# An earlier first modulation round and normed input inside the memory projection of a two-block kernel

## The chip, the cores and the metric

The kernel runs on one core of a Trainium2 chip. The metric is the device time of one execution in microseconds (us). Five engines work side by side and meet only at semaphores: TensorE (PE in the rows, its weight loads as PEld), VectorE (DVE), ScalarE (ACT), GpSimd (POOL) and SyncE (SP), which here only issues DMAs. The issue of a DMA shows as SPq, ACTq or POOLq.

## The reference, cut to what matters

Two transformer-like blocks on 512 positions of width 1024. What the change touches is the start of block 1 and a piece of block 2 that doesn't depend on block 1:

```python
cond = silu(c)
mod = cond @ ada_w + ada_b                       # 6 rows of 1024: sh1, sc1, g1, sh2, sc2, g2
u = rms_norm(x, mix_pre_g) * (1.0 + sc1) + sh1   # 512 x 1024, the mixer's normed input
proj = u @ w_in                                  # convolution branch first: a, gate
y = causal_dwconv(a * sigmoid(gate), cv_dw_w)    # 31 taps
...
m = rms_norm(mem, mem_norm_g)                    # block 2: 256 memory tokens
kv = m @ cross_w_kv                              # 1024 x 2048: keys and values of the cross-attention
```

All weights are float32. Products keep nearly float32 accuracy with three matmuls in a reduced type: a weight and an activation are each split into a high part and the low rest, and high by high, high by low and low by high are added up.

## The kernel before, in words

The first stage of the program is `memory` (L426, phase name `mem`). It reads the memory's weight `w_kv` in 16 chunks of 512 KB, c0 to c15 here, in four units of four chunks. A chunk is loaded by `weight` (L131): SP loads it into a buffer `raw` (three of them), ScalarE casts the high part (L140), VectorE subtracts for the low part (L146), both into a buffer of tag `whl` (four of them). Then TensorE does 12 matmuls of 128x512 (`mm3`, L151 to L153). L151 needs the high part of the weight; in this stage L152 is the one that needs its low part. After units 0 and 1 TensorE also transposes the keys (L486, tile `kn`), and each unit's result goes to DRAM by a DMA on POOL's queue (L498, `kvd`).

After each chunk the function `weave` (L538) is called with the chunk's number. It places the preparation of the mixer among the chunks:

- One step of `ada_round(0, ...)` (L236), the first modulation round: two tiles of 512 KB of `ada_w` (`aw`, four buffers, so two steps' worth) are loaded by SP and multiplied on TensorE in four small fp32 matmuls (L254; eight in the trace). There are eight steps, r0 to r7. After r7 VectorE adds `ada_b` (L257).
- `x_load(tb)` (L509): one of four blocks of x is loaded by SP, ScalarE sums its squares (L207), VectorE and POOL take the root, VectorE scales it (L515), TensorE transposes it (L520) and it is put into `xT`.
- `norm1()` (L528): transposes of the modulation (`mod_cols`, L264), then for each of eight slices of the features a scaling on VectorE (L534), a cast to the high part on ScalarE (L193) and the low part on VectorE (L194). The result is `u`, split; in the rows it is `mem_U`.

Next comes the mixer (L630), phase `glu`: 16 weight chunks g0 to g15 of `w_in`, each a `weight` and 24 matmuls in `fm_tile` (L215). In the mixer `lowdma` is set, and `weight` takes another way to the low part: ScalarE casts the high part (L140), writes minus the high part (L142), and a DMA on POOL's queue adds the raw weight to that (L143). Only when this accumulating DMA has landed is the low part there, and only then is the `raw` buffer free. In `fm_tile` it is L153 that needs the low part. A round of modulation for later use (`glu_U`) is woven into this phase too, and the 31-tap convolution runs on VectorE behind it.

The order of instructions on each engine is not the order of the source: a scheduling framework orders them by its own model of durations, and decides which buffer of a tag a tile gets. On an engine the order is then fixed, and what waits holds up everything behind it. SP's queue is one such order: a load that waits for its buffer holds up the loads behind it.

```python
ada = self.ada_round(0, lambda: pz.tile([P, 1024], F32, tag="aw", bufs=4, ...))   # L524
...
mm(out, lh, rh, start=start, stop=False)     # L151
mm(out, lh, rl, start=False, stop=False)     # L152
mm(out, ll, rh, start=False, stop=stop)      # L153
...
nc.scalar.activation(w[:, 1], raw, AF.Copy, scale=-1.0)            # L142, in the mixer
nc.gpsimd.dma_start(out=w[:, 1], in_=raw, accum_op=ALU.add)        # L143
```

Of the kernel before, what the change touches and what calls it, by code (L numbers as in the profile page):

```python
# [46 lines left out]
class Kern:  # L47
# [15 lines left out]
    def setup(self):  # L63
        nc, tc, ctx = self.nc, self.tc, self.ctx
        self.p0 = ctx.enter_context(tc.tile_pool(name="p0", bufs=1))
        self.psp = ctx.enter_context(tc.tile_pool(name="psp", bufs=4, space=PSUM))
        self.dr = ctx.enter_context(tc.tile_pool(name="dr", bufs=1, space=bass.MemoryType.DRAM))
        self.cols = self.p0.tile([P, self.a["cols"].shape[1]], F32, tag="cols", name="cols")
        nc.sync.dma_start(self.cols, self.a["cols"])
        self.ident = self.p0.tile([P, P], F32, tag="ident", name="ident")  # L70
        make_identity(nc, self.ident)
        self.ones = self.p0.tile([P, P], F32, tag="ones", name="ones")
        nc.vector.memset(self.ones, 1.0)
        self.half = self.p0.tile([P, 4], F32, tag="half", name="half")
        nc.vector.memset(self.half, -0.5)

        self.p0.tile([P, 8], F32, tag="mcol", bufs=2, name="mcol")
        self.p0.tile([P, 8], F32, tag="cvec", name="cvec")
        self.p0.tile([P, 8], F32, tag="cond", name="cond")
        self.p0.tile([P, 112], F32, tag="gap0", name="gap0")  # L80
# [142 lines left out]
    def ada_setup(self):  # L223
        nc = self.nc
        c = self.p0.tile([P, 8], F32, tag="cvec", name="cvec")
        nc.sync.dma_start(c, self.a["c"])
        cond = self.cond = self.p0.tile([P, 8], F32, tag="cond", name="cond")
        nc.scalar.activation(cond, c, AF.Silu)
        self.misc = self.p0.tile([P, 2048], F32, tag="misc", name="misc")
        self.crep = self.misc[:, 1024:1280].rearrange("p (k c) -> p k c", k=8)  # L230
        self.sin = self.misc[:, 1280:1664].rearrange("p (t f) -> p t f", t=4)
        self.cos = self.misc[:, 1664:2048].rearrange("p (t f) -> p t f", t=4)
        nc.vector.tensor_copy(self.crep, cond.unsqueeze(2).to_broadcast([P, 8, 32]))
        self.mods = {}
# [266 lines left out]
    def block1(self):  # L501
        nc, tc, a = self.nc, self.tc, self.a
        self.ada_setup()
        with tc.tile_pool(name="pz", bufs=1) as pz:
            self.phase = "mem"
            xT = self.U(F32)
            xs, xi = [], []

            def x_load(tb):  # L509
                t = pz.tile([P, 1024], F32, tag="x", bufs=2, name=f"x{tb}")  # L510
                nc.sync.dma_start(t, a["x"][tb * P:(tb + 1) * P, :])
                ss = self.small(1)
                self.sumsq(t, ss)
                rs = self.rsqrt(ss, D)
                nc.vector.tensor_scalar(t, t, rs, None, op0=ALU.mult)  # L515
                for i in range(2):
                    ps = self.psB()
                    for k in range(4):
                        kk = i * 4 + k
                        nc.tensor.transpose(ps[:, k * P:(k + 1) * P], t[:, kk * P:(kk + 1) * P], self.ident)  # L520
                    (nc.scalar.copy if i else nc.vector.tensor_copy)(
                        xT[:, i * 4:i * 4 + 4, 0, tb * P:(tb + 1) * P], ps.rearrange("p (k t) -> p k t", k=4))

            ada = self.ada_round(0, lambda: pz.tile([P, 1024], F32, tag="aw", bufs=4, name=self.nm("aw")))  # L524

            u = self.U()

            def norm1():  # L528
                self.phase = "norm1"
                sh1 = self.mod_col8(0, 0)  # L530
                g1 = self.mod_col8(0, 1, "mix_pre_g")
                for k in range(8):
                    t = self.tB()
                    nc.vector.tensor_scalar(t, xT[:, k, 0], g1[:, k:k + 1], sh1[:, k:k + 1], op0=ALU.mult, op1=ALU.add)  # L534
                    self.split(u[:, k, 0], u[:, k, 1], t)
                self.phase = "mem"

            def weave(i):  # L538
                if i in (0, 2, 3, 5, 7, 9, 11, 13):
                    next(ada, None)  # L540
                if i in (3, 5, 7, 9):
                    x_load((3, 5, 7, 9).index(i))
                if i == 15:
                    norm1()

            self.memory(pz, weave)
        with tc.tile_pool(name="pa", bufs=1) as pa:
            mix, g1row, sh2, g2p = self.mixer(pa, u)
        with tc.tile_pool(name="pf", bufs=1) as pf:
            self.phase = "wout"  # L550
            self.pf = pf
            u2 = pf.tile([P, 8, 2, 512], F32R, tag="U2", name="u2")
            self.xs = []
            for tb in range(4):
                t = pf.tile([P, 1024], F32, tag="x4", bufs=6, name=self.nm("x"))
                nc.sync.dma_start(t, a["x"][tb * P:(tb + 1) * P, :])
                self.xs.append(t)
            self.xd = self.dr.tile([S, D], F32, tag="xd", bufs=2, name=self.nm("xd"))

            def after(tbs, ps):  # L560
                self.spill(tbs)
                return self.prenorm(tbs, self.xs, u2, ps, gcol=g2p, shcol=sh2)

            self.fin = self.post(g1row, after)
            for later in mix:
                pass
            self.phase = "up"
            act = self.ffn(pf, u2, later)
            self.phase = "down"
            self.rope_tables()  # L570
            self.clear_rows()
            g2row = self.mod_row(pf.tile([P, 1024], F32, tag="row1", name="g2row"), 2, 1, "ffn_post_g")
            an = self.row(pf, "attn_norm_g", tag="row2")
            xt = pf.tile([P, 8, 1024], F32, tag="U2", name="xt")
            self.xs = [xt[:, tb] for tb in range(4)]
            for tb in range(4):
                nc.sync.dma_start(self.xs[tb], self.xd[tb * P:(tb + 1) * P, :])
            self.xd = self.dr.tile([S, D], F32, tag="xd", bufs=2, name=self.nm("xd"))
            self.hA = None

            def after(tbs, ps):
                if self.hA is None:
                    self.hA = self.U()
                self.spill(tbs)
                return self.prenorm(tbs, self.xs, self.hA, ps, grow=an)

            for self.later in self.wide_product(act, "ffn_down", NFF, (((0, 1), 0, 8), ((0,), 8, 22), ((1,), 8, 22)),
                                                self.post(g2row, after)):
                pass
# [1606 lines left out]
```

## Time and profile before

| what | us |
|---|---|
| median of 3 runs (lowest, highest) | 1535.51 (1530.5, 1536.32) |
| the profiled execution, its own time | 1530.15 |
| its span, first to last instruction | 1528.4 |
| TensorE busy in the span | 1459.3 |
| VectorE, ScalarE, GpSimd busy | 958.8, 671.2, 124.4 |

The span is a little shorter than the execution's time, since launch and end lie around it. All stages named above lie in the first 100 us of the span; the rest of the program (mixer, feed-forward, attention, experts) follows them one after the other. Times of rows count from the span's start. A row of the timeline has the start, the duration, the engine, the line, the operation with what it writes and reads, how many instructions were merged, and in brackets how long the engine had been idle and what released it. Matmuls are pipelined, so their distance is shorter than the duration a row shows.

### The profile page before, as it was taken

The page shows a single profiled execution, that of the slowest core. Times are in us where ns is not written, and L with a number is a line of the kernel's source. Part 1 is how long each engine was busy: PE and PEld are TensorE (multiplying, and loading weights), DVE is VectorE, ACT ScalarE, POOL GpSimd, SP SyncE. Part 2 cuts the span into 40 slices and gives each one's busy share as a digit, 9 for nine tenths or more (in the row PEclk, how much of TensorE's full clock was granted, in tenths as well). Part 3 has the DMA queues.
Part 4 walks back from the last instruction along what each step waited for, and adds up shares of the span by engine and source line. Part 5 has one row for each costly group of instructions (what it writes and reads, how often), then busy time and mean ns, then how long its engine had stood idle before and what let it go on. Part 6 is the DMA issues. An engine that isn't in the chain of part 4 may idle for free.

```text
span 1528.4 us, 19917 instructions
## 1 busy us (share of the span) xinstructions
PE 1459.3 (95%) x7096; PEld 1083.4 (71%) x7096; DVE 958.8 (63%) x2099; ACT 671.2 (44%) x1212; POOL 124.4 (8%) x152
## 2 busy tenths in 40 slices
PE   7989999999999999999999999999999998999886
PEld 5667778778788788888888877878878785333322
DVE  4569999994866866565524778775676557332114
ACT  5553486576755754444324554454354421111010
POOL 0111111111000000000000010000011001111100
PEclk9999999999999999999999999999999999999999
DMA  9899977876376553333425633242343667999997
GB/s 333 308 287 270 272 183 189 225 193 151 111 262 206 179 194 96 97 96 97 145 90 193 200 125 111 93 163 90 97 151 102 232 250 283 416 412 412 409 410 282
DMA packets 95767, 321.66 MB, mean 210 GB/s; under 512 B 13129, under 2 KB 13641, under 8 KB 95664
## 3 DMA queue, kind: packets, MB, share of 16 engines
q1 hardware_dynamic: 80832, 276.39, 51.4%
q0 software_dynamic: 11952, 35.56, 10.5%
q10 hardware_dynamic: 2880, 8.39, 1.4%
q8 instruction: 57, 0.93, 0.2%
q14 instruction: 46, 0.38, 0.1%
HBM read 275.83 MB, written 26.74 MB: 198 GB/s over the span
## 4 chain that ended last, share of the span: by engine, by line
PE 69%; DMA 15%; DVE 9%; ACT 3%; issue 2%; POOL 2%; SPq 0%; ACTq 0%; DVEq 0%; POOLq 0%
PE up_pa L152 5%; PE up_pa L153 5%; PE up_pa L151 5%; PE glu_pa L151 2%; PE glu_pa L152 2%; PE vo_pa L151 2%; PE glu_pa L153 2%; PE vo_pa L153 2%; PE vo_pa L152 2%; PE wout_pa L153 2%; PE wout_pa L151 2%; PE wout_pa L152 2%; DMA wo_U<-in_w_dn_dram 2%; DMA crossq_U<-in_w_gu_dram 2%; DMA moe_U<-in_w_gu_dram 2%
## 5 line engine op out<-in xcount | busy, mean ns | idle before, releaser
L648 DVE SCALAR_TENSOR_TENSOR y<-g,cols,y 128x493 f32<-128x493 f32 (+26 forms) x240 | 165.7, 729 | 5.5 <-ACT y L645 3.8
L152 PE MATMUL up_pa<-u,up_w 128*128 128x512 f32 (+1 forms) x384 | 142.6, 372 | 0.4 <-DVE u L194 0.4
L151 PE MATMUL up_pa<-u,up_w 128*128 128x512 f32 (+1 forms) x384 | 142.3, 372 | 0.3 <-ACT u L193 0.3
L153 PE MATMUL up_pa<-u,up_w 128*128 128x512 f32 (+1 forms) x384 | 142.5, 372 | 0.0
L936 DVE SCALAR_TENSOR_TENSOR up_tA<-up_pa,cols,up_tA 128x511 f32<-128x511 f32 x88 | 65.8, 749 | 72.2 <-ACT up_tA L934 70.8
L151 PEld LDWEIGHTS up_pa<-u,up_w 128*128 128x128 f32 x384 | 72.1, 188 | 13.7 <-ACT u L193 1.1
L152 PEld LDWEIGHTS up_pa<-u,up_w 128*128 128x128 f32 x384 | 72.3, 188 | 13.0 <-DVE u L194 0.6
L153 PEld LDWEIGHTS up_pa<-u,up_w 128*128 128x128 f32 x384 | 72.3, 188 | 12.5
L146 DVE TENSOR_TENSOR down_w<-down_raw,down_w 128x1024 fp32r<-128x1024 f32 x36 | 42.8, 1220 | 55.3 <-ACT down_w L140 55.3
L1782 DVE COPY moe_xT<-moe_pb 128x512 f32<-128x512 f32 x15 | 10.4, 691 | 105.7 <-PE moe_pa L1896 105.3
L146 DVE TENSOR_TENSOR wout_w<-wout_raw,wout_w 128x512 fp32r<-128x512 f32 (+1 forms) x72 | 51.3, 745 | 35.2 <-ACT wout_w L140 35.0
L140 ACT CAST down_w<-down_raw 128x1024 fp32r<-128x1024 f32 x36 | 36.6, 1051 | 64.2 <-PE down_pb L153 33.0
L140 ACT CAST wout_w<-wout_raw 128x512 fp32r<-128x512 f32 (+1 forms) x72 | 44.8, 670 | 44.2 <-PE wout_pa L153 23.7
L934 ACT ACTIVATE up_tA<-up_pa,cols 128x512 f32<-128x512 f32 x44 | 34.4, 781 | 67.8 <-PE up_pa L153 67.7
L1898 ACT ACTIVATE moe_sl<-moe_pa,moe_gt 128x256 f32<-128x256 f32 x16 | 7.6, 474 | 124.1 <-PE moe_pa L1896 124.1
L151 PE MATMUL glu_pa<-mem_U,glu_w 128*128 128x512 f32 x128 | 51.6, 406 | 3.8 <-ACT mem_U L193 3.8
L146 DVE TENSOR_TENSOR up_w<-up_raw,up_w 128x1024 fp32r<-128x1024 f32 (+1 forms) x48 | 54.0, 1127 | 0.1
L152 PE MATMUL glu_pa<-mem_U,glu_w 128*128 128x512 f32 x128 | 51.4, 403 | 0.4 <-DVE mem_U L194 0.4
L152 PE MATMUL g_pa<-g_w,down_U 128*128 128x512 f32 x128 | 51.0, 399 | 0.5 <-DVE g_w L146 0.5
L151 PE MATMUL g_pa<-g_w,down_U 128*128 128x512 f32 x128 | 51.3, 402 | 0.0
L153 PE MATMUL glu_pa<-mem_U,glu_w 128*128 128x512 f32 x128 | 50.8, 398 | 0.0
L153 PE MATMUL g_pa<-g_w,down_U 128*128 128x512 f32 x128 | 50.7, 396 | 0.0
(758 smaller groups left out, 3950.0 us busy)
## 6 DMA issues: line engine op xcount, KB each, us to landing
up_raw<-in_ffn_up_dram SPq DMA_DIRECT2D x44, 512.0 KB
wout_raw<-in_w_out_dram SPq DMA_DIRECT2D x40, 512.0 KB
ew<-in_w_gu_dram SPq DMA_DIRECT2D x39, 512.0 KB
down_raw<-in_ffn_down_dram SPq DMA_DIRECT2D x36, 512.0 KB
glu_U<-in_ada_w_dram SPq DMA_DIRECT2D x32, 512.0 KB
moe_ew<-in_w_gu_dram SPq DMA_DIRECT2D x19, 512.0 KB
mem_raw<-in_w_kv_dram SPq DMA_DIRECT2D x16, 512.0 KB
mem_aw<-in_ada_w_dram SPq DMA_DIRECT2D x16, 512.0 KB
```

The costliest lines, as they stand in the source:

```text
L140: nc.scalar.copy(w[:, 0, c], raw[:, c])
L146: nc.vector.tensor_tensor(w[:, 1, c], raw[:, c], w[:, 0, c].bitcast(F32), op=ALU.subtract)
L151: mm(out, lh, rh, start=start, stop=False)
L152: mm(out, lh, rl, start=False, stop=False)
L153: mm(out, ll, rh, start=False, stop=stop)
L648: nc.vector.scalar_tensor_tensor(acc[:, s:], g[:, :512 - s], cw[:, j:j + 1], acc[:, s:], op0=ALU.mult, op1=ALU.add)
L934: nc.scalar.activation(acc, pq, AF.Identity, scale=cwv(2), bias=self.col("ffn_conv_b", cc))
L936: nc.vector.scalar_tensor_tensor(acc[:, s:], pq[:, :512 - s], cwv(2 - s), acc[:, s:], op0=ALU.mult, op1=ALU.add)
L1782: (nc.scalar.copy if i else nc.vector.tensor_copy)(t[:, i * 4:i * 4 + 4].rearrange("p k c -> p (k c)"), ps)
L1898: nc.scalar.activation(sl, ps[:, :256], AF.Silu, scale=s["gt"][:, 2:3])
```

## The change

Five lines change. The constants `cols` (per-channel vectors) and the vector c are loaded by DMAs on ScalarE's queue, no longer SP's. In `weave` the eight modulation steps stand after c0, c1, c2, c3, c5, c6, c8 and c9 (before: c0, c2, c3, c5, c7, c9, c11, c13), the four blocks of x after c2, c4, c6 and c7 (before: c3, c5, c7, c9), and the normed input after c11 (before: c15).

```diff
-        nc.sync.dma_start(self.cols, self.a["cols"])
+        nc.scalar.dma_start(self.cols, self.a["cols"])
...
-        nc.sync.dma_start(c, self.a["c"])
+        nc.scalar.dma_start(c, self.a["c"])
...
             def weave(i):
-                if i in (0, 2, 3, 5, 7, 9, 11, 13):
+                if i in (0, 1, 2, 3, 5, 6, 8, 9):
                     next(ada, None)
-                if i in (3, 5, 7, 9):
-                    x_load((3, 5, 7, 9).index(i))
-                if i == 15:
+                if i in (2, 4, 6, 7):
+                    x_load((2, 4, 6, 7).index(i))
+                if i == 11:
                     norm1()
```

The order of the engines changes with it, in this first part of the program only; behind the first glu chunks it is the same on all engines. TensorE at the end of the memory stage, before the change (`mem_w_679` is c15; `glu_w_758`, `_791` and `_849` belong to g0, g1 and g2):

```order
L152 MATMUL mem_pa_616<-mem_w_679,mT 128x512
L153 MATMUL mem_pa_616<-mem_w_679,mT 128x512
L264 MATMUL norm_pb_694<-ident,misc 128x128 x4
L264 MATMUL norm_pb_701<-ident,misc 128x128 x4
L151 MATMUL glu_pa_762<-mem_U_89,glu_w_758 128x512
L151 MATMUL glu_pa_795<-mem_U_89,glu_w_791 128x512
L151 MATMUL glu_pa_849<-mem_U_89,glu_w_845 128x512
L152 MATMUL glu_pa_762<-mem_U_89,glu_w_758 128x512
L153 MATMUL glu_pa_762<-mem_U_89,glu_w_758 128x512
```

And TensorE with the change, at c14 (`mem_w_708`):

```order
L153 MATMUL mem_pa_671<-mem_w_691,mT 128x512
L151 MATMUL mem_pa_670<-mem_w_708,mT 128x512
L151 MATMUL mem_pa_671<-mem_w_708,mT 128x512
L151 MATMUL glu_pa_762<-mem_U_89,glu_w_758 128x512
L152 MATMUL glu_pa_762<-mem_U_89,glu_w_758 128x512
L153 MATMUL glu_pa_762<-mem_U_89,glu_w_758 128x512
L151 MATMUL glu_pa_762<-mem_U_89,glu_w_758 128x512
L152 MATMUL mem_pa_670<-mem_w_708,mT 128x512
L153 MATMUL mem_pa_670<-mem_w_708,mT 128x512
```

The modulation's transposes have gone from behind c15 to c10 and c11, and four matmuls of g0, the low part's L153 among them, now stand between the first two matmuls of c14 and its other ten; c15 follows these.

ScalarE with the change, around the first glu weight (`mem_w_708` and `mem_w_725` are c14 and c15, `mem_U_89` and `mem_U_90` the two halves of the normed input):

```order
L140 CAST mem_w_708<-mem_raw_706 128x1024
L140 CAST mem_w_725<-mem_raw_723 128x1024
L193 CAST mem_U_89<-norm_tB_634 128x512
L193 CAST mem_U_89<-norm_tB_638 128x512
L193 CAST mem_U_89<-norm_tB_642 128x512
L193 CAST mem_U_89<-norm_tB_646 128x512
L140 CAST glu_w_758<-glu_raw_756 128x1024
L142 ACTIVATE glu_w_758<-glu_raw_756 128x1024
```

Before, the two passes of g0's weight stood behind the cast of c15 and ahead of all casts of the normed input; now the first four of these come first.

SP with the change, around the loads of the first glu weights (in brackets the semaphores that a DMA waits for; `DMASW3` is the accumulating DMA of g0):

```order
L136 DMA glu_raw_756<-in_w_in_dram 128x1024 [waits DMAHW3_49,DVE_49]
L243 DMA misc<-in_ada_b_dram 32x512 [waits DMAHW1_49,PE_49]
L243 DMA misc<-in_ada_b_dram 32x512 [waits DMAHW2_49]
L243 DMA misc<-in_ada_b_dram 32x512
L243 DMA misc<-in_ada_b_dram 32x512 [waits DMAHW4_49]
L1765 DMA early<-in_w_gu_dram 128x1024 [waits DMAHW5_49]
L251 DMA glu_U_755<-in_ada_w_dram 128x1024 [waits DMAHW6_49,DVE_49]
L251 DMA glu_U_755<-in_ada_w_dram 128x1024 [waits DMAHW7_49]
L136 DMA glu_raw_789<-in_w_in_dram 128x1024 [waits DMAHW0_49,DMASW3_49,Activation_49]
L136 DMA glu_raw_843<-in_w_in_dram 128x1024 [waits DMAHW1_49,DVE_49]
L136 DMA glu_raw_876<-in_w_in_dram 128x1024 [waits DMAHW2_49,DVE_49]
```

Before, it was the fourth glu weight (`glu_raw_876`) that took over g0's raw buffer and waited for that accumulating DMA; now it is the second (`glu_raw_789`), with the third and the fourth queued behind it.

## Rows read from the trace of the kernel before

**Rows 1.** The page's part 1: busy us, share of the span, instructions.

```profile
PE 1459.3 (95%) x7096; PEld 1083.4 (71%) x7096; DVE 958.8 (63%) x2099; ACT 671.2 (44%) x1212; POOL 124.4 (8%) x152
```

**Rows 2.** Chain that ended last, 76 to 99 us: start us, us, what ran.

```profile
79.97 6.21 DMA glu_raw<-in_w_in_dram
86.27 1.04 ACT glu_w L140
87.32 0.53 ACT mem_U L193
...
88.50 0.43 PE glu_pa L152
...
98.45 0.23 PE glu_pa L153
```

**Rows 3.** Stretches of 2 us: busy us by engine, then PE clock, DMA share, GB/s.

```profile
12.00:14.00 2.00, 2.00 (x6) 1.34 (x6) 2.00 (x5) 0.90 (x4) 0.00 (x0) 1.00 1.03 422
...
48.00:50.00 2.00, 2.00 (x12) 1.68 (x10) 2.00 (x4) 1.44 (x5) 0.00 (x0) 1.00 0.46 115
...
80.00:82.00 2.00, 1.65 (x6) 1.22 (x6) 2.00 (x4) 1.69 (x3) 0.00 (x0) 0.82 1.04 244
82.00:84.00 2.00, 2.00 (x6) 1.51 (x6) 2.00 (x5) 0.00 (x0) 0.00 (x0) 0.50 0.97 254
84.00:86.00 2.00, 1.61 (x6) 0.95 (x4) 0.12 (x1) 0.00 (x0) 1.05 (x3) 0.82 1.04 361
```

**Rows 4.** Timeline of SP's queue, 0 to 100 us.

```profile
0.81 0.38 SPq L69 DMA_DIRECT2D cols<-in_cols_dram  x1
1.24 0.42 SPq L226 DMA_DIRECT2D cvec<-in_c_dram  x1
1.71 0.90 SPq L432 DMA_DIRECT2D m<-in_mem_dram  x2
...
18.86 0.80 SPq L251 DMA_DIRECT2D mem_aw<-in_ada_w_dram  x2
19.71 0.42 SPq L511 DMA_DIRECT2D x<-in_x_dram  x1
...
79.97 0.33 SPq L136 DMA_DIRECT2D glu_raw<-in_w_in_dram  x1
```

**Rows 5.** Timeline of TensorE, 17 to 97 us.

```profile
17.77 1.06 PE L254 MATMUL mem_pb<-mem_aw,misc 128*32 128x512 f32 x8
...
29.36 1.09 PE L520 MATMUL mem_pb<-ident,x 128*128 128x128 f32 x8
...
63.44 1.07 PE L254 MATMUL mem_pb<-mem_aw,misc 128*32 128x512 f32 x8
...
76.69 1.03 PE L264 MATMUL norm_pb<-ident,misc 128*128 128x128 f32 x8
...
96.64 0.39 PE L153 MATMUL glu_pa<-mem_U,glu_w 128*128 128x512 f32 x1
```

**Rows 6.** Timeline of ScalarE, VectorE and POOL, 3 to 81 us.

```profile
3.80 0.21 ACT L228 ACTIVATE cond<-cvec 128x8 f32<-128x8 f32 x1 [1.71 <-DMA cvec<-in_c_dram]
...
25.68 1.06 ACT L207 ACTIVATE mem_jk<-x 128x1024 bf16<-128x1024 f32 x1 [4.85 <-DMA x<-in_x_dram]
...
74.91 0.90 POOL L143 DMA_DIRECT2D glu_w<-glu_raw  x1 [9.32 <-ACT glu_w L142]
...
76.60 0.67 ACT L497 ACTIVATE mem_kv<-mem_pa,mem_sm 128x512 f32<-128x512 f32 x1
...
77.96 1.92 DVE L534 TENSOR_SCALAR norm_tB<-mem_U,norm_mcol,norm_mcol 128x512 f32<-128x512 f32 x4
78.54 2.18 ACT L193 CAST mem_U<-norm_tB 128x512 fp32r<-128x512 f32 x4 [0.34 <-DVE norm_tB L534]
...
79.80 2.49 DVE L194 TENSOR_TENSOR mem_U<-norm_tB,mem_U 128x512 fp32r<-128x512 f32 x4
```

**Rows 7.** The accumulating DMAs (tile glu_w, 60 to 110 us), issue to landing.

```profile
DMA to landing us min/median/max: 5.0/6.1/7.1
```

## The prediction

> **What bounds the kernel now.** I read the page's part 1 first: TensorE is busy for 1459.3 of 1528.4 us [rows 1], so time comes only from gaps of TensorE, or from time at its lower clock. The change touches the first 100 us, so next I read the chain that ended last across the hand-over from the memory stage to the glu phase [rows 2]. There the chain leaves TensorE: 6.21 us for the load of a glu weight, 1.04 us for its cast, 0.53 us for a cast of the normed input that stood behind it on ScalarE, and only then matmuls. Those come 0.43 us apart, against 0.23 us ten us later. The stretches say why: the granted clock is 0.82, 0.50 and 0.82 in the three from 80 to 86 us [rows 3], which is a mixture of the full level (2.4 GHz) and the lower one (1.2 GHz), after TensorE had stopped and waited. The normed input is late because it can't begin before the modulation's transposes at 76.69 [rows 5], behind the last memory chunk. The last matmul of g1 starts at 96.64 [rows 5], so g0 and g1 are through at 97.0. Their 48 matmuls take 11 us at 0.23 us each [rows 2]; between 77.7, when the transposes are done, and 97.0 lie 19.3 us. About 8 us are there to be had, no more, and that is the whole of 0.5% of the kernel.
>
> The DMA engines matter as well. In the memory stage their share is often full (1.03 at 422 GB/s), but not always (0.46 at 115 GB/s) [rows 3]: SP then holds back a load whose buffer isn't free.
>
> **The change part by part.** The sum goes to one point, the end of g1, 97.0 before. Behind it the order of all engines is the old one, each stage waits for the one ahead of it, and what is won or lost there is carried to the end.
>
> *Constants on ScalarE's queue.* SP issued them at 0.81 and 1.24 and the memory tokens at 1.71 [rows 4]. The tokens now go first: 0.90 us earlier. ScalarE issues the two instead, and is idle until 3.80 [rows 6]. Ends: 0, if the DMA engines are the limit and the bytes come in the same time anyway, and 1.5, if the transposes of the tokens, which now follow one another, save some 0.6 us more (an estimate: a bit over half of one modulation step's 1.06 us [rows 5]). I take 0.90, the row.
>
> *Modulation and x among c0 to c11.* The work is the same, so each step that comes earlier is paid where it lands: by the end of c11 there are two more modulation steps, 1.06 us each, and the transposes of `mod_cols`, 1.03 us [rows 5]. They are missing later. What is new is a wait. A modulation step can be loaded only when the step two before it has left its `aw` buffers: r2's load follows the start of r0 by 18.86 - 17.77 = 1.09 us, and the x block behind it is issued 19.71 - 17.77 = 1.94 us after that start [rows 4, 5]. That x block is transposed 29.36 - 19.71 = 9.65 us after its issue [rows 4, 5]; 5.97 us of this is the load (25.68) [rows 6], the rest sums, root and scaling. Before, c1, c2 and c3 lay in between; now only c1 and c2 do. With r0 at 17.77 - 0.90 = 16.87, x0 is transposed at 16.87 + 1.94 + 9.65 = 28.46. From there I use the stretch before, which has the same eight chunks c4 to c11, four x blocks and three modulation steps in it: 63.44 - 29.36 = 34.08 us to the end of c11 [rows 5]. To that add eleven matmuls of c3 (2.53), two steps (2.12) and `mod_cols` (1.03). So c11 ends at T = 28.46 + 34.08 + 5.68 = 68.2 (before: 63.44). Ends: 65, if x0 comes in time and no load is waited for, and 69.5, if the later pairs, also two steps behind, cost one more wait like it.
>
> *The normed input after c11.* VectorE and ScalarE do it beside c12 to c15: two halves of 1.92 + 2.49 us on VectorE [rows 6], under matmuls. It costs nothing as long as TensorE has those chunks to do. But here the new order decides, not the source: TensorE does c12, c13 and two matmuls of c14 (26 x 0.23 = 6.0 us, at T + 6.0), two of g0 (T + 6.4), and then stands at g0's L153, which needs the accumulating DMA. That comes late. ScalarE, after c11, has the evacuation (0.67), the casts of c14 and c15 (1.04 each), four casts of the normed input (2.18), and only then g0's two passes (1.04 each) [rows 2, 6]: 6.9 us if nothing else delays it. The DMA is issued at T + 6.9 and lands a us later. For a, the first one before took from 74.91 to 79.97, when SP was released by it [rows 4, 6], and the shortest, middle and longest are 5.0, 6.1 and 7.1 [rows 7]. I take 5.0: the first one, at the same place. So TensorE waits from T + 6.4 to T + 11.9, 5.5 us, with ten matmuls of c14, all of c15 and the rest of g0 queued behind L153 and able to run. **The old wait for the normed input is gone; a wait for g0's low part stands in its place.**
>
> After it: two matmuls of g0, 22 of c14 and c15, 20 of g0 (44 x 0.23 = 10.1), and once more the lower clock as above, 2 x (0.18 + 0.50 + 0.18) = 1.7 us [rows 3]: T + 23.7, and two matmuls into g1 at T + 24.2. g1's low part is late too. Its raw load now takes over g0's buffer and waits until the first accumulating DMA has landed, T + 11.9; then 6.3 us for load and queue (79.97 to 86.27) [rows 2], 2.1 us of passes, and a second accumulating DMA of 5.0: T + 25.3. TensorE waits 1.1 us, then needs 22 x 0.23 = 5.06 us: g1 ends at T + 30.4. In general, while this chain decides, it is T + 20.4 + 2a.
>
> *Sum.* 68.2 + 30.4 = 98.6 against 97.0: 1.6 us later. Against the profiled execution's 1530.15 that is 1531.7; the median of the runs lies 5.4 us higher, so **1537**. What lies beyond the chain is covered: the second half of the normed input (VectorE) and the low parts of c14 and c15 end while TensorE waits for g0; the third and fourth glu loads follow the second by one issue each and have a chunk's time, 5.5 us, more.
>
> *Ends of a.* The trace of before has no accumulating DMA with otherwise idle DMA engines. Below: the 4 KB vector took 3.80 - 1.24 = 2.6 us from issue to use [rows 4, 6], and 0.524 MB at 422 GB/s are 1.2 us [rows 3]: 3.8. Above: 7.1 [rows 7]. The Trainium skill, "DMA: Bandwidth & Descriptors", section "Anatomy of one DMA — SWDGE (gpsimd) path", fits such a DMA with 2.0 us plus bytes at 436 GB/s, which would be 3.2 us here as an estimate; by it the sum would come to about 1534. No row of this trace is that short.
>
> **Rivals.**
>
> *The wait shrinks (faster).* The DMA engines are nearly idle while SP waits for g0's accumulating DMA, so a is 3.8, and x0 comes in time, T = 65. Then the chain and TensorE's own work arrive together: 65 + 20.4 + 7.6 = 93.0, 4.0 us earlier: 1531.5. For it: idle DMA engines. Against it: two `glu_U` tiles and an expert tile stand ahead of g1's load and move just then. The fit of the Trainium skill named above would speak for it as well.
>
> *The accumulating DMAs crawl (slower).* Beside those three tiles a is 7.1, the longest of the phase. Then 68.2 + 20.4 + 14.2 = 102.8, 5.8 us later: 1541. It decides from a = 3.8 upwards, where the chain passes TensorE's own work, and the result turns slower than before at T + 2a above 76.6. For it: the middle of the phase is 6.1. Against it: glu weights no longer queue up beside the first one.
>
> *It doesn't do what it says.* x or the modulation comes so late that the normed input isn't begun at c11. Then the old wait stays and the time is the old one, 1535. The order has `mod_cols` at c10, so only late data could do it.
>
> **How the numbers follow.** Forecast 0.55, shrinking wait 0.20, crawling DMAs 0.20, nothing done 0.05. 0.5%, about what a measurement of this kernel can tell from no change, is 7.7 us. Neither faster nor slower rival reaches it alone: faster would need the full 8 us above, slower T = 69.5 with a = 7.1 (104.1, 7.1 us later) and a bit of scatter. So faster 0.07, same 0.84, slower 0.09. The range goes from the shrinking wait with 2 us of scatter, 1529, to the crawling DMAs with T = 69.5, 1543.
>
> **What would show it.** Right: TensorE idle for 4 to 7 us at a g0 L153 in the middle of c14, released by `glu_w`, a granted clock near 0.5 behind it, g1's load issued when that DMA lands, no wait for `mem_U`, and g1's end between 95 and 101. Right for the start: the memory tokens issued at 0.8; a wait of TensorE for x in c3. Wrong: no such wait in c14 (then a gain near 8 us), c11 ending before 64 or after 70, or a difference that appears behind 100 us.

## The result, and the profile after

| | before | after |
|---|---|---|
| median of 6 runs each, us | 1533.23 (1530.5 to 1536.32) | 1542.31 (1538.46 to 1543.57) |
| ratio to before, 95% interval | | 1.0059 (1.0045 to 1.0073) |
| profiled execution, span, us | 1530.15, 1528.4 | 1538.46, 1536.7 |
| end of g1 | 97.0 | 106.4 |

The changed kernel is 9.1 us slower. That is clear of zero, and 0.59% lies just beyond the 0.5% that bounded "same"; the interval, 0.45% to 0.73%, reaches to both sides of that bound. All of it arises in the first 106 us: g1 ends 9.5 us later (the modulation step behind it starts at 106.43 instead of 96.95), and three hundred microseconds on, the transposes of `ynorm` are 9.4 us later (412.4 against 403.0). TensorE's instructions and its busy time are those of before, as the page shows [rows 1]:

```profile
PE 1459.6 (95%) x7096; PEld 1081.3 (70%) x7096; DVE 958.8 (62%) x2099; ACT 670.9 (44%) x1212; POOL 123.4 (8%) x152
```

The chain that ended last across the hand-over, in the changed kernel (start us, us, what ran), answers to [rows 2]:

```profile
68.59 5.74 DMA mem_raw<-in_w_kv_dram
...
74.43 1.05 ACT mem_w L140
75.48 1.63 ACT mem_U L193 x4
...
77.47 1.04 ACT glu_w L140
78.50 0.97 ACT glu_w L142
...
79.77 6.72 DMA glu_w<-glu_raw
...
86.54 3.60 DMA glu_raw<-in_w_in_dram
...
91.20 1.07 ACT glu_w L142
...
92.55 8.62 DMA glu_w<-glu_raw
...
101.22 0.50 PE glu_pa L153
```

The piece shown starts with the raw load of c15, passes through the casts of the normed input's first half to the passes of g0's weight, and then consists of DMAs: g0's accumulating DMA (6.72), g1's raw load, which had waited for it, and g1's accumulating DMA (8.62). TensorE at these places, where [rows 5] has those of before; brackets give the idle time and who ended it:

```profile
17.84 1.07 PE L254 MATMUL mem_pb<-mem_aw,misc 128*32 128x512 f32 x8
19.50 1.05 PE L254 MATMUL mem_pb<-mem_aw,misc 128*32 128x512 f32 x2
22.97 1.06 PE L254 MATMUL mem_pb<-mem_aw,misc 128*32 128x512 f32 x6
...
29.42 1.04 PE L520 MATMUL mem_pb<-ident,x 128*128 128x128 f32 x8
...
70.85 0.38 PE L264 MATMUL norm_pb<-ident,misc 128*128 128x128 f32 x2
...
78.56 0.50 PE L151 MATMUL glu_pa<-mem_U,glu_w 128*128 128x512 f32 x1 [1.39 <-ACT glu_w L140]
...
86.53 0.80 PE L153 MATMUL glu_pa<-mem_U,glu_w 128*128 128x512 f32 x1 [7.24 <-DMA glu_w<-glu_raw]
...
101.22 0.50 PE L153 MATMUL glu_pa<-mem_U,glu_w 128*128 128x512 f32 x1 [1.91 <-DMA glu_w<-glu_raw]
```

The forecast wait is there, in the middle of c14: 7.24 us before g0's L153. The granted clock behind it is 0.50, the 1.2 GHz level, until about 91 us (stretches of 2 us, columns as in [rows 3]):

```profile
82.00:84.00 2.00, 0.00 (x0) 0.00 (x0) 2.00 (x4) 0.00 (x0) 0.00 (x0) 0.50 0.93 211
...
86.00:88.00 2.00, 1.47 (x4) 1.18 (x5) 0.00 (x0) 0.00 (x0) 0.00 (x0) 0.50 0.76 279
...
90.00:92.00 2.00, 2.00 (x8) 1.54 (x8) 0.00 (x0) 1.76 (x2) 0.00 (x0) 0.76 1.01 393
```

The 9.5 us have two parts. **The memory stage**: c11 ends at T = 70.85, and c12 to c15 still need 48 x 0.227 = 10.9 us, so the stage's work would be done at 81.8 without a wait; before, with the modulation's transposes, it was done at 77.7. That is 4.1 us. On TensorE it can be counted: three modulation steps are cut in two, and each cut costs a second row of about 1 us (x2 and x6 above, for two of them); and TensorE's waits up to T add up to 12.5 us, against 11.2 in the whole stage before. **The hand-over**: from there to g1's end it is 24.6 us, before 19.3: 5.3 us. The waits in it are 1.39 + 7.24 + 1.91 = 10.5 us, against 1.49 + 0.35 + 2.28 = 4.1 us before:

```profile
79.21 0.97 PE L151 MATMUL glu_pa<-mem_U,glu_w 128*128 128x512 f32 x3 [1.49 <-ACT mem_U L193]
80.54 0.50 PE L152 MATMUL glu_pa<-mem_U,glu_w 128*128 128x512 f32 x1 [0.35 <-DVE mem_U L194]
...
87.89 0.61 PE L151 MATMUL glu_pa<-mem_U,glu_w 128*128 128x512 f32 x1 [2.28 <-ACT mem_U L193]
```

The waits alone would be 6.4 us more. About 1 us of that comes back at the clock: 16 matmuls of the hand-over stood 0.43 us apart before, 10 stand so now.

That the weights come late is to be seen on SP and on ScalarE. SP's waits from 0 to 72 us (us in total, times, longest), after and then before:

```profile
SPq L251 <- PE mem_pb L254: 22.3, 6, 7.8
```

```profile
SPq L251 <- PE mem_pb L254: 10.3, 2, 5.9
```

SP stands 12 us longer at a modulation load whose `aw` buffer is not free, with the memory chunks' loads queued behind it. From 60 to 64 us the DMA engines moved 394 GB/s before and 148 now. That this wait of SP makes the weights late isn't shown, and two runs below speak against it: in e6 it is halved (11.6 us) and the weights are as late; in e8 it is longer (24.7 us) and the casts of c14 and c15, at 67.34 and 69.81, are 2.5 us behind those of the kernel before and not 6 to 7. The changed kernel, e1 and e6, all with late weights, have another thing in common: at 59 us ScalarE casts three memory chunks in a row behind a cast for the keys, which has waited for VectorE; in the kernel before two such casts stand there, at 54.73. SP's next raw loads need the buffers of these chunks (a wait for L146 of up to 6.9 us, before 4.5). No run took that order apart. ScalarE's casts then show the collision, in the changed kernel and behind it in the kernel before:

```profile
57.55 1.57 ACT L479 ACTIVATE mem_kn<-mem_pa,mem_sm 128x256 f32<-128x256 f32 x4 [1.78 <-DVE mem_sm L474]
58.99 2.95 ACT L140 CAST mem_w<-mem_raw 128x1024 fp32r<-128x1024 f32 x3
...
70.96 1.04 ACT L140 CAST mem_w<-mem_raw 128x1024 fp32r<-128x1024 f32 x1
74.43 1.05 ACT L140 CAST mem_w<-mem_raw 128x1024 fp32r<-128x1024 f32 x1 [2.44 <-DMA mem_raw<-in_w_kv_dram]
75.38 2.18 ACT L193 CAST mem_U<-norm_tB 128x512 fp32r<-128x512 f32 x4
77.47 1.04 ACT L140 CAST glu_w<-glu_raw 128x1024 fp32r<-128x1024 f32 x1
```

```profile
64.71 1.05 ACT L140 CAST mem_w<-mem_raw 128x1024 fp32r<-128x1024 f32 x1 [0.21 <-DMA mem_raw<-in_w_kv_dram]
67.41 1.05 ACT L140 CAST mem_w<-mem_raw 128x1024 fp32r<-128x1024 f32 x1 [1.65 <-DMA mem_raw<-in_w_kv_dram]
72.59 1.05 ACT L140 CAST glu_w<-glu_raw 128x1024 fp32r<-128x1024 f32 x1 [4.13 <-DMA glu_raw<-in_w_in_dram]
```

The casts of c14 and c15 moved from 64.71 and 67.41 to 70.96 and 74.43, that of g0 from 72.59 to 77.47. The normed input came 3 us sooner (78.54 before, [rows 6]) and now stands ahead of weights that come 5 to 7 us later. On VectorE the same: the low parts of c14 and c15 run last, behind the whole normed input:

```profile
82.68 2.35 DVE L146 TENSOR_TENSOR mem_w<-mem_raw,mem_w 128x1024 fp32r<-128x1024 f32 x2
```

### The profile page after: what moved, and what is told of

It is laid out like the page before. It is cut to its first block, busy times and chain, and to the rows that moved or that the text cites. A ratio compares the mean times of both kernels' runs of the same rounds, so it can differ in the third digit from the quotient of the medians.

```text
span 1536.7 us, 19920 instructions
## 1 busy us (share of the span) xinstructions
PE 1459.6 (95%) x7096; PEld 1081.3 (70%) x7096; DVE 958.8 (62%) x2099; ACT 670.9 (44%) x1212; POOL 123.4 (8%) x152
## 4 chain that ended last, share of the span: by engine, by line
PE 75%; DVE 9%; DMA 9%; ACT 3%; issue 2%; POOL 2%; ACTq 0%; DVEq 0%; POOLq 0%; SPq 0%
PE up_pa L152 5%; PE up_pa L153 5%; PE up_pa L151 5%; PE moe_pa L1896 5%; PE moe_pa L1922 2%; PE glu_pa L151 2%; PE vo_pa L151 2%; PE wout_pa L153 2%; PE glu_pa L153 2%; PE wout_pa L151 2%; PE vo_pa L153 2%; PE vo_pa L152 2%; PE wout_pa L152 2%; PE glu_pa L152 2%; PE qk_pa L152 1%
## 5 line engine op out<-in xcount | busy, mean ns | idle before, releaser
L153 PE MATMUL up_pa<-u,up_w 128*128 128x512 f32 (+1 forms) x384 | 142.5, 372 | 0.0
L153 PEld LDWEIGHTS up_pa<-u,up_w 128*128 128x128 f32 x384 | 72.3, 188 | 12.3
L146 DVE TENSOR_TENSOR down_w<-down_raw,down_w 128x1024 fp32r<-128x1024 f32 x36 | 42.8, 1221 | 55.4 <-ACT down_w L140 55.4
L146 DVE TENSOR_TENSOR wout_w<-wout_raw,wout_w 128x512 fp32r<-128x512 f32 (+1 forms) x72 | 51.4, 746 | 35.1 <-ACT wout_w L140 35.0
L153 PE MATMUL glu_pa<-mem_U,glu_w 128*128 128x512 f32 x128 | 50.4, 394 | 9.1 <-DMA glu_w<-glu_raw 9.1
L146 DVE TENSOR_TENSOR up_w<-up_raw,up_w 128x1024 fp32r<-128x1024 f32 (+1 forms) x48 | 54.1, 1127 | 0.3 <-ACT up_w L140 0.3
L151 PE MATMUL glu_pa<-mem_U,glu_w 128*128 128x512 f32 x128 | 51.0, 398 | 1.4 <-ACT glu_w L140 1.4
L153 PE MATMUL g_pa<-g_w,down_U 128*128 128x512 f32 x128 | 50.7, 396 | 0.0
L151 PE MATMUL qk_pa<-mem_U,qk_w 128*128 128x512 f32 x128 | 50.1, 391 | 0.0
## 6 DMA issues: line engine op xcount, KB each, us to landing
ew<-in_w_gu_dram SPq DMA_DIRECT2D x39, 512.0 KB, 10.9
moe_ew<-in_w_gu_dram SPq DMA_DIRECT2D x19, 512.0 KB, 11.2
```

The source lines that it names most:

```text
L146: nc.vector.tensor_tensor(w[:, 1, c], raw[:, c], w[:, 0, c].bitcast(F32), op=ALU.subtract)
```

## The experiments

Each was timed beside the kernel before on the same chip. A difference is median minus the median of before there: 1531.24 for e1 to e4, 1531.45 for e5 to e8, 1531.32 for e9 to e11, 1530.62 for e12. The intervals are 3 to 6 us wide, so smaller steps are read from the end of g1 in the traces: 106.4 in the changed kernel, 97.0 before. `issue_after` fixes the order of instructions on one engine and adds no wait. e1 to e6 and e9 start from the changed kernel, the others from the kernel before.

**e1: no modulation step cut in two.** The order lets other matmuls in between the four strips of a step.

```diff
+                with self.tc.issue_after(self.last) if r == 0 else ExitStack():
+                    for j in range(4):
...
```

> The changed kernel, with the four matmuls of each step of the first modulation round tied behind the last matmul of the weight chunk ahead of them, so that TensorE's order has each step in one piece (in the changed kernel three of the eight steps are cut in two, one matmul here and three there). Theory A (a step in pieces costs more: a row of 2 records takes 1.05 us and a row of 6 takes 1.06, as long as all 8 in one piece): three steps times about 1 us come back before the end of c11, which then ends near 68 instead of 70.9, and the time is 2 to 3 us below the changed kernel's 1542.3, so 1539 to 1540. Rival B (TensorE has to wait for the data anyway, the pieces cost nothing): 1542. In both the wait for g0's accumulating DMA stays.

1540.76, +9.5 us, ratio 1.0073 (1.0055 to 1.0091). TensorE of e1:

```profile
42.50 0.50 PE L152 MATMUL mem_pa<-mem_w,mT 128*128 128x512 f32 x1 [1.20 <-DVE mem_w L146]
...
58.28 0.33 PE L487 MATMUL mem_pb<-ident,mem_kn 128*128 128x128 f32 x1 [1.57 <-ACT mem_kn L480]
...
71.14 1.03 PE L265 MATMUL norm_pb<-ident,misc 128*128 128x128 f32 x8
```

The steps run whole, yet c11 ends at 71.14: TensorE waits where it had worked on cut steps, 16.0 us up to T in place of 12.5, for casts and low parts of weights, for x and for the keys. Rival B holds; the time lost before T is set by what TensorE waits for. In this trace g1 ends at 110.2, later than in the changed kernel: the wait for g1's low part is 2.64 us here in place of 1.91, and behind it the granted clock is 0.50 from 102 to 108 us, where it stayed at 1.00 in the changed kernel.

**e2: nothing of g0 ahead of c14 and c15.**

```diff
-            pg = self.fm_tile(u, self.weight(W[2 * c]), self.psA())
+            with self.tc.issue_after(self.last) if c == 0 else ExitStack():
+                pg = self.fm_tile(u, self.weight(W[2 * c]), self.psA())
```

> The changed kernel, with all matmuls of g0 tied behind the last matmul of c15: the four matmuls of g0 that stood inside c14 are back behind c15, nothing else moves. Theory A (g1's chain decides: its raw load waits for the buffer that g0's accumulating DMA reads, then load, two passes, second accumulating DMA): that chain doesn't touch TensorE, g1 still ends near 106 and the time stays 1541 to 1542.5, although the 7.2 us wait in c14 becomes shorter or moves. Rival B (the forecast's picture of the wait in c14 as the price): about 5 to 7 us faster than the changed kernel, 1535 to 1537.

1540.97, +9.7, ratio 1.0069 (1.0055 to 1.0083). Its TensorE:

```profile
83.58 0.79 PE L152 MATMUL mem_pa<-mem_w,mT 128*128 128x512 f32 x1 [6.16 <-DVE mem_w L146]
...
100.91 0.50 PE L153 MATMUL glu_pa<-mem_U,glu_w 128*128 128x512 f32 x1 [4.08 <-DMA glu_w<-glu_raw]
```

Theory A held: the wait only changes its name, now for the low part of c14 that VectorE makes behind the normed input. My picture of matmuls of c14 "queued behind L153 and able to run" was wrong for most of the wait; c14's low part wasn't there until 84. g1's end comes no sooner (107.75).

**e3: g1's raw load in a buffer of its own** (a half of `xT` that is free then); **e4: e2 and e3 together.**

```diff
+        self.spare = self.Uh(F32)
+        self.turn_u -= 1
...
-            pv = self.fm_tile(u, self.weight(W[2 * c + 1]), self.psA())
+            raw = self.spare.rearrange("p a b n -> p a (b n)")[:, 0] if c == 0 else None
+            pv = self.fm_tile(u, self.weight(W[2 * c + 1], raw=raw), self.psA())
```

> The changed kernel, with the raw weight of g1 loaded into space that the blocks of x have left, instead of g0's raw buffer: its load needn't wait for g0's accumulating DMA. Theory A (two things in a row, each enough alone): TensorE still stands in c14 until that DMA lands at about 86.5 and then has 44 matmuls of c14, c15 and g0 and 24 of g1 to do; only the 1.9 us wait in g1 goes, g1 ends near 104.4, 1540 to 1541. Rival B (the buffer is the whole price): 1533 to 1535. Rival C (more traffic beside g0's accumulating DMA makes that slower still): 1542 or more.

> Both edits of the two kernels before it: g0's matmuls behind c15, and a raw buffer of its own for g1. Theory A (the two are in series, only both together free TensorE): then c14's low part is next, which VectorE makes behind the whole normed input (83.8 in the changed kernel), so that c14 and c15 end near 91, g0 near 96.5 and g1 near 102: 4 to 5 us below the changed kernel, 1537 to 1538.5. Rival B (each saves its own part, and the parts simply add): the sum of what the two kernels before it save. Rival C: no better than the better of the two.

e3: 1538.3, +7.1, ratio 1.0046 (1.0033 to 1.0059), g1's end 104.25. e4: 1537.02, +5.8, ratio 1.0035 (1.0022 to 1.0048), g1's end 101.87. Theory A held in both at g1's end; the gain in time, 2.0 and 3.3 us against the changed kernel's +9.1, is a little smaller than it said for e4, and that of e3 isn't clear of noise (the changed kernel's interval begins at 1.0045). The profiled execution of e3 took 1544.91, its other four 1537.8 to 1538.8, so only g1's end is read from it. The waits lie one behind the other: removing the first alone gives nothing, the second alone 2.2 us at g1's end, both 4.5.

**e5: quiet DMA engines around the first accumulating DMAs.** The loads of `glu_U` and of the first two expert tiles go behind g5's load on SP, and modulation round 1 is taken some pairs later.

```diff
-            next(ada)
+            with self.tc.issue_after(self.load):
+                for _ in range((0, 0, 2, 1, 1, 1, 1, 2)[c]):
+                    next(ada)
```

> The changed kernel (9 us slower than before on the same chip), with the loads of the second modulation round and of the first two expert tiles tied on SP behind the load of g5, so that only glu weights move while the first accumulating DMAs run. Theory A (the accumulating DMAs are long because other loads share the DMA engines): the first takes 4 to 5 us in place of 6.7, the second 6 to 7 in place of 8.6, g1 ends 3 to 4 us earlier than 106.4, the time is 5 to 6 us above before. Rival B (they are long by themselves): both stay within 0.7 us of 6.7 and 8.6, the time stays 8 to 9 us above before.

Chain of e5:

```profile
79.45 4.44 DMA glu_w<-glu_raw
...
83.96 3.54 DMA glu_raw<-in_w_in_dram
...
89.90 5.59 DMA glu_w<-glu_raw
```

The first accumulating DMA takes 4.44 us instead of 6.72, and the second 5.59 instead of 8.62: neighbours on the DMA engines make them long. The 48th matmul of the glu phase starts at 102.00 instead of 106.11, so theory A held as far as g1's end. The time is 1546.25 all the same, +14.8, ratio 1.0097 (1.0082 to 1.0111): the postponed loads come due later (5.3 us of waits for `glu_U` after 105 us, 1.7 us for low parts, a granted clock of 0.89 from 190 to 220 us), and `ynorm` is at 421.0.

**e6: six `aw` buffers instead of four** (room from `kvo`, two instead of four).

> The changed kernel, with six aw buffers in place of four (three modulation steps' worth; the memory's result staging has two buffers in place of four to make room). Theory A (the memory stage ends late because SP waits 22.3 us in six waits for aw buffers and holds back the weight and x loads behind them): these waits fall below 12 us, the waits of TensorE for casts and splits in c4 and for the keys go, c11 ends at 67 to 69 in place of 70.9, and the time is 5.5 to 7 us above before, in place of 9. Rival B (the DMA engines or VectorE are the limit anyway): c11 ends at 70 to 71, 8 to 9 us above before.

1542.73, +11.3, ratio 1.0075 (1.0062 to 1.0088). SP's waits from 0 to 72 us in e6:

```profile
SPq L136 <- DVE mem_w L146: 20.5, 9, 6.9
SPq L251 <- PE mem_pb L254: 11.6, 3, 5.4
```

The wait for `aw` is halved, and SP waits for raw buffers instead. The end of c11 doesn't move (70.96), rival B, and TensorE's waits up to there are the 12.6 us of the changed kernel. The casts of c14 and c15 are as late (71.06 and 73.82). The time is above rival B's 8 to 9 us; the two `kvo` buffers less may have a part in that, which no run separates. The steps were still cut in this run; e1 and e6 together were not tried, so what sets T is open.

**e7: the kernel before with the constants on ScalarE's queue alone** (the two lines of the diff).

> The kernel before, with only the two constants on ScalarE's queue, no step moved. Theory A (the memory tokens come 0.9 us sooner but the constants 2 to 3 us later, and r0 starts at the same 17.8): the time is that of before within 1 us either way. Rival B (the forecast's term): 0.9 us faster than before, r0 at 16.9. Rival C (late constants cost): 2 us or more slower than before.

1530.6, -0.9, ratio 0.9995 (0.9986 to 1.0004). The first transpose of the tokens comes at 5.41, but the first modulation step at 19.00 instead of 17.77; in this trace the matmuls ahead of it stand 0.43 us apart from 15.4 to 18.4, which they don't in the changed kernel. Theory A held for the time, though not for r0's 17.8: nothing clear of noise.

**e8: the same purpose without the delays.** The kernel before with dense steps late in the stage, the normed input after c11, no cut steps, and g0 behind c15.

```diff
-                if i in (0, 2, 3, 5, 7, 9, 11, 13):
+                if i in (0, 2, 3, 5, 7, 8, 10, 11):
...
-                if i == 15:
+                if i == 11:
...
```

> A try at a better version: the kernel before, constants on SP, x after c3, c5, c7, c9 as before, modulation steps after c0, c2, c3, c5, c7, c8, c10, c11 (only the last three earlier), the normed input after c11, each modulation step in one piece and all of g0 behind c15. Theory A (the early normed input is worth having if the steps ahead of it don't hold up SP, if VectorE makes c15's low part before most of it, and if g1's load has a free buffer): the memory stage ends near 78, g0's low part lands at 80 to 82, g1 ends near 93, 3 to 5 us faster than before. Rival B (packing two more steps ahead of c11 already holds up SP's loads): the memory stage ends at 81 or later, and the time is that of before within 2 us, or slower.

1534.33, +2.9, ratio 1.0023 (1.0014 to 1.0033). TensorE of e8:

```profile
82.25 0.50 PE L153 MATMUL glu_pa<-mem_U,glu_w 128*128 128x512 f32 x1 [2.21 <-DMA glu_w<-glu_raw]
...
94.14 1.07 PE L255 MATMUL glu_pb<-glu_U,misc 128*32 128x512 f32 x8
...
109.00 0.50 PE L153 MATMUL glu_pa<-mem_U,glu_w 128*128 128x512 f32 x1 [1.03 <-DMA glu_w<-glu_raw]
...
123.94 0.50 PE L153 MATMUL glu_pa<-mem_U,glu_w 128*128 128x512 f32 x1 [2.55 <-DMA glu_w<-glu_raw]
```

g1 ends 2.8 us sooner than in the kernel before, with the normed input as early as in the changed one. So the early normed input by itself is not what costs: here the casts of c14 and c15 stand ahead of it. But 1.03 and 2.55 us of new waits follow at 109 and 124, and `ynorm` is 3.8 us later: with three raw buffers, each held until an accumulating DMA has landed, the weights now set the pace, as e10 below bears out in the main.

**e9 to e11: low parts of g0 to g3 on VectorE**, as the memory's, instead of by accumulating DMA; e9 in the changed kernel, e10 in e8, e11 in the kernel before.

```diff
-        self.lowdma = True
+        self.lowdma = False
...
+            self.lowdma = c >= 2
```

> The changed kernel (9 us slower than before), with the low part of g0 to g3 made by a subtraction on VectorE, as for the memory's weights, instead of the accumulating DMAs; everything else as the change has it, from g4 on as well. Theory A (the accumulating DMAs are what the early hand-over waits for): TensorE waits in c14 only until VectorE has made c14's low part behind the normed input (about 84), c14 and c15 end near 91, g0 near 96.5, g1 near 102; raw buffers come free at once, so nothing is given back later: 4 to 5 us above before. Rival B (the late memory stage is the whole loss): 8 to 9 us above before. Rival C (all of the loss): within 1.5 us of before.

> The denser version (steps after c0, c2, c3, c5, c7, c8, c10, c11, normed input after c11, steps in one piece, g0 behind c15), which reached g1's end 2.9 us sooner than before and then lost 6.7 us to late low parts, with the low parts of g0 to g3 on VectorE. Theory A (the accumulating DMAs with three raw buffers set the pace of the first glu chunks, so an earlier hand-over alone finds the weights not ready): the memory stage ends near 78.7, VectorE has g0's low part at about 80.5 and g1's at 82, g1 ends at 91.7 to 93, the next pairs follow at 12.1 us each, and the time is 3.5 to 5 us below before. Rival B (VectorE is now late with the normed input and with the convolution behind it, or the loads can't keep up): same as before within 1.5 us. Rival C: slower by 2 us or more.

> The kernel before, with the low parts of g0 to g3 on VectorE and nothing moved: the control for the kernel ahead of this one. Theory A (before, the normed input was the wait, not the low parts): TensorE still waits for casts of the normed input behind c15, g1 ends at 95.5 to 97 and the time is that of before within 1.5 us. Rival B (the low parts alone are the gain, the early normed input isn't needed): 3 us or more faster than before.

| | median, us | difference | ratio, interval | g1's end | `ynorm` |
|---|---|---|---|---|---|
| e9 | 1536.08 | +4.8 | 1.0033 (1.0021 to 1.0045) | 101.56 | 407.5 |
| e10 | 1527.15 | -4.2 | 0.9974 (0.9965 to 0.9983) | 92.17 | 400.6 |
| e11 | 1524.88 | -6.4 | 0.9957 (0.9944 to 0.9970) | 91.69 | 397.9 |

e9 and e10 came as theory A said. e9 wins 4 to 5 us, but e11 wins 6.4 with the same edit, so on this footing too the change costs 11.2 us (e9 against e11). In e9 TensorE still waits 4.05 us for the low part of c14. So the accumulating DMA lengthens the wait, but the change costs as much without it. In e10 2.4 us are lost between g1 and `ynorm`, where e8 lost 6.6; it isn't ahead of e11.

e11 was the surprise, rival B. The wait of 2.28 us at 87.89 in the kernel before came from ScalarE, where the casts of the normed input stood behind a cast of g3's weight:

```profile
86.27 1.04 ACT L140 CAST glu_w<-glu_raw 128x1024 fp32r<-128x1024 f32 x1 [4.59 <-DMA glu_raw<-in_w_in_dram]
87.22 2.17 ACT L193 CAST mem_U<-norm_tB 128x512 fp32r<-128x512 f32 x4
```

And g3's raw load stood behind g0's accumulating DMA, which held the buffer until 79.97 [rows 2, 4]. In e11 that cast is at 81.08, without a wait, and the one long stop is gone:

```profile
81.08 1.05 ACT L140 CAST glu_w<-glu_raw 128x1024 fp32r<-128x1024 f32 x1
...
83.22 1.66 ACT L193 CAST mem_U<-norm_tB 128x512 fp32r<-128x512 f32 x3 [1.10 <-DVE norm_tB L534]
```

**e12: e11 with the normed input after c13** (`i == 13`).

> The kernel before with the low parts of g0 to g3 on VectorE (6.4 us faster than before), and one thing moved: the normed input after c13, where the last modulation step stands, in place of c15. Theory A (moving the normed input alone, behind the low parts of c14 and c15 on VectorE and without packing the modulation steps, is a gain): the remaining waits of 1.5 and 0.3 us at the start of g0 go or shrink, the memory stage still ends near 78, g1 ends at 90 to 91 in place of 91.7, and the time is 7.5 to 8.5 us below before. Rival B (VectorE and ScalarE are then late with what stands behind, and the wait moves): 5.5 to 7 us below before. Rival C (an early normed input costs): less than 5 us below before.

1524.93, -5.7, ratio 0.9964 (0.9951 to 0.9978): the time is rival B's, g1's end is better than theory A's. TensorE has no wait at the hand-over at all:

```profile
77.76 0.61 PE L151 MATMUL glu_pa<-mem_U,glu_w 128*128 128x512 f32 x2
...
88.89 1.06 PE L254 MATMUL glu_pb<-glu_U,misc 128*32 128x512 f32 x8
```

g1 ends 8.1 us sooner than in the kernel before, the whole that the prediction said was to be had, and `ynorm` is 8.2 us sooner. In the time, 5.7 us are left; where the rest goes after 395 us I didn't follow, and e11 and e12 can't be told apart by their times. The casts of c14 and c15 are at 66.42 and 68.93 here, 1.5 to 1.7 us behind those of the kernel before, and their low parts are done before the normed input begins on VectorE at 74.5.

## Where the prediction held and where it failed

The place and the main mechanism were right. The old wait for the normed input went away; a wait at g0's L153 in the middle of c14 took its place; the clock fell behind it; g1's load was issued when that DMA landed; behind 106 us nothing is lost (by the spans about 1 us comes back). 1542.3 lies in the range, near its upper end. The sign was right; the size, +1.6 against +9.1, was not, and 0.84 stood on "same", of which the result lies just outside. The base lay 2.3 us too high (1535.51, three runs, against 1533.23, six), so the forecast misses by 5.3 us where the change was misjudged by 7.5. That the result is in the range is owed to this luck: counted from its own base, the range ended at 7.5 us later. Three signs that the prediction set itself failed as well: c11 ended after 70, which it had named as wrong, g1 ended behind 101, and TensorE had no wait for x in c3.

| step of the sum | forecast | measured |
|---|---|---|
| constants: all 0.90 us earlier | r0 at 16.87 | 17.84 |
| end of c11, T | 68.2 | 70.85 |
| g0's accumulating DMA issued | T + 6.9 | T + 8.9 |
| its a | 5.0 | 6.72 |
| raw load of g1 with its queue | 6.3 | 3.7 |
| a of g1 | 5.0 | 8.62 |
| 22 matmuls | 5.06 | 5.2 |
| g1's end | 98.6 | 106.4 |

- *Constants on ScalarE's queue: 0.90.* Fell. The tokens do go first, but c then lands later: ScalarE waited for it 1.7 us before [rows 6] and 4.1 us now, and its sums over the tokens, which stand behind, begin at 7.20 instead of 6.24. The first matmul of c0 still came 0.8 us sooner (10.88 against 11.70); then TensorE waited 1.25 us for VectorE's part of the transposed tokens, which it did not before, and the lead was gone by the first modulation step. e7 has the same two waits and no gain in time.
- *"Each step that comes earlier is paid where it lands."* Fell in part. I counted TensorE's time and one wait of SP, and let the loads and casts of the memory chunks run as before. T was 2.6 us later than forecast. 0.97 us of that is r0's, above; x0 was transposed 11.6 us behind r0, as forecast. Behind x0 one step is cut in two (about 1 us), and TensorE waits 2.6 us in place of the 1.7 of the stretch that I took over. Neither whole steps (e1) nor six `aw` buffers (e6) bring it back. And the weights of c14, c15 and g0 were 5 to 7 us later than before; what made them late stays open.
- *ScalarE: 6.9 us behind c11.* It was 8.9: the cast of c15 waited 2.44 us for its raw load, the same lateness once more. With the weights late, the normed input got ahead of g0's passes on ScalarE and of the low parts of c14 and c15 on VectorE. The prediction let those low parts end while TensorE waits for g0, and they did (85.0 against 86.5), but that hid a second wait, 6.16 us in e2: with "it costs nothing as long as TensorE has those chunks to do" I had not asked when TensorE could do them. e2 (the wait changes its name), e8 and e12 (early normed input, weights in time, little or no wait) show this side of it.
- *a = 5.0.* The largest error, 1.7 and 3.6 us. I took the first one's row at the same place. There SP's last load, an expert tile, had been issued at 70.18, 4.7 us ahead of it, and the next came when it had landed. In the changed kernel two `glu_U` tiles follow 0.6 us behind the first one, and raw loads, `glu_U` and an expert tile stand in the 6 us ahead of the second:

```profile
80.39 0.82 SPq L251 DMA_DIRECT2D glu_U<-in_ada_w_dram  x2
86.54 1.28 SPq L136 DMA_DIRECT2D glu_raw<-in_w_in_dram  x3
```

The share of the DMA engines alone doesn't give the length: it was 0.99 during the first one before (5.06 us) and 0.81 now (6.72 us). The "crawl" rival had the right reason, as e5 shows, and even its 7.1 was too low for the second. Landing of all accumulating DMAs from 60 to 110 us in the changed kernel [rows 7]:

```profile
DMA to landing us min/median/max: 6.7/8.6/11.2
```

- *g1's end is T + 20.4 + 2a.* Held in form: 70.85 + 20.4 + 6.72 + 8.62 = 106.6, measured 106.4. The late issue (+2.0) and the shorter raw load (-2.6) nearly cancel, so that it comes out so close is partly luck.
- *About 8 us are to be had.* Held in size: e12 had 8.1 at g1's end. The reason that I named, the modulation behind the last chunk, is the smaller part: e11, with the modulation left where it was, has 5.3 of the 8.1 from the raw buffer that g0's accumulating DMA holds, and in the time no run shows a gain beyond e11's 6.4.

## What to carry to other kernels

Work that is moved forward takes its loads and its passes with it: before counting the gain, lay the loads and the passes of each engine out in their new order and see which weights come later, and what those late weights then stand behind on the engines that prepare them. Follow a wait back past the engine that is named as its releaser to the buffer that was not free: here that led from a cast of the normed input to a DMA that held a raw buffer, and giving that DMA's work to VectorE for four weights saved 6.4 us without moving anything else. Waits in a row have to be removed together; one alone may show nothing.

## What the runs showed of the hardware

An accumulating DMA of 0.5 MB took 4.44 us nearly alone (e5: the DMA engines moved 118 GB/s meanwhile, which is its own 0.52 MB), 6.7 to 11.2 in the changed kernel, and 5.0 to 7.1 in the kernel before [rows 7]. By the Trainium skill, "DMA: Bandwidth & Descriptors", section "Anatomy of one DMA — SWDGE (gpsimd) path", it would be 3.2 us as an estimate (2.0 us and the bytes at 436 GB/s); that fit is for a DMA of this path in general, and no run here comes near it with one that accumulates.

A modulation step is four strips of 32 partitions. All four together took 1.07 us (the row x8 at 17.84), three 1.06 (x6) and one alone 1.05 (x2): the strips run side by side, and a step that is cut in two pays twice. The Trainium skill, "TensorEngine Tiling (Array Packing)", section "Key Properties", says that tiles operate independently and can execute in parallel; the rows agree.
